# A product of the first MLP group is computed second, in a bank of its own, and operands read from PSUM are cut first

## The chip, the core and the metric

One core of a Trainium2 chip runs the whole kernel. The metric is the device time of one execution in microseconds (us); lower is better. Three runs of the kernel before gave 2158.07, 2158.14 and 2159.57 us; the median, 2158.14 us, is its time.

## What is computed

An encoder layer on 1536 tokens (512 and 1024) of width 1024: two kinds of attention, a gated merge, and an MLP with a squared ReLU. The change touches only the way into the MLP and its first product, `hn @ W_up`:

```python
hn = _rmsnorm(h, norm_mlp_g[l])
h = h + jnp.square(jax.nn.relu(hn @ w_mlp_up[l])) @ w_mlp_down[l]
```

All products are float32. The kernel writes each operand x as a rounded part hi and a remainder lo = x - hi, and adds three products, hi·hi + hi·lo + lo·hi (`mm3`, lines 190 to 193: L191, L192 and L193 in the profile).

## The kernel before

**Blocks and groups.** The MLP takes the tokens in two blocks of 768. For each block it runs through 16 groups of 256 hidden units. Within a group the product of a 2 by 2 block of weights with a 2 by 2 block of activations is built from seven smaller products instead of eight (Strassen's scheme in Winograd's form). The weights' halves are a11, a12, a21, a22 (`up_steps`, lines 1257 to 1284). From them and from the sums S0 to S3 come seven left operands A0 to A6, each cut into hi (L1212, on ScalarE, called ACT in the profile) and lo (L1213, on VectorE, called DVE). The right operands B0 to B6 are made once for a block by `pair_t` and stay for all its 16 groups.

**`pair_t`** (lines 310 to 349) makes three times 128 columns of B0 to B6. TensorE (PE) transposes two tiles of normalised activations into four PSUM banks (`pt`, L315). Two tiles of two banks each serve `pt` in the first block, and the next call's transposes must wait until the banks of the call before have been read for the last time. B0, B4 and B5 are bank contents as they stand (b11, b22, b21). B1, B2, B3 and B6 come from the differences a2, a1, a3, a4, which VectorE computes into SBUF (`ta`; L335, L334, L338, L340). y1 (L332) is a copy of the bank b12. `hi` (L324) rounds on ScalarE. `lo` (L327) subtracts on VectorE, for B2 and B6 on GpSimd (POOL). For the first block the three calls stand between the last matmuls of the output projection (`ops`), whose results also go to memory (`xrs`, L1149 on VectorE and L1150, a DMA that GpSimd issues).

**`up`** (lines 1292 to 1352) runs a group. Each of the seven products is 12 matmuls of 128x128 by 384 columns and adds into one of four PSUM banks, `ua`, `ub`, `uc`, `ud`. Their order is 0, 1, 2, 3, 4, 6, 5. Products 4, 6 and 5 are added onto a bank that held an earlier product, so they may start only when that one has been read: product 4 goes onto product 2's bank `uc` after s5 (L1343, ScalarE) has been copied from it, product 6 onto product 3's bank `ud` after L1330 (VectorE) has added it to s5, and product 5 onto product 0's bank `ua` after s1 (L1339) was copied. `put` adds (L1330), takes the ReLU and the square (L1331, L1332 on ScalarE) and stores. After each product `step` issues a share of the cuts for the next group (`side`).

**What sets the order.** The code is recorded, and a scheduler then places the instructions of each engine; what stands in one engine's queue is executed in that order. Loads are issued by SyncE (SP). The pool that holds A's cut operands (`k4`) lies where the projection's tiles lay, so a new tile of it may have to wait for the last use of what lay there, also for a store of `xrs` to land.

Of the kernel before, what the change touches and what calls it, by code (L numbers as in the profile page):

```python
# [15 lines left out]
ALU = mybir.AluOpType  # L16
# [14 lines left out]
HB = BT // 2  # L31
# [30 lines left out]
def encoder(ctx: ExitStack, tc: tile.TileContext, xs, outs, w):  # L62
    nc = tc.nc
# [126 lines left out]
    def mm3(out, ah, al, bh, bl, start, stop, **kw):  # L190
        nc.tensor.matmul(out, ah, bh, start=start, stop=False, **kw)  # L191
        nc.tensor.matmul(out, ah, bl, start=False, stop=False, **kw)  # L192
        nc.tensor.matmul(out, al, bh, start=False, stop=stop, **kw)  # L193
# [116 lines left out]
    def pair_t(nm, j, tiles, B, banks, tmp):  # L310

        b11, b21, b12, b22 = banks
        for halves, t in (((b11, b21), tiles[0]), ((b12, b22), tiles[1])):
            for c in range(NC8):
                nc.tensor.transpose(  # L315
                    halves[c // 4][:, (c % 4) * P : (c % 4 + 1) * P], t[:, c * P : (c + 1) * P], ident
                )
        cols = slice(j * P, (j + 1) * P)

        def v(t):  # L320
            return t.rearrange("p (k c) -> p k c", c=P)

        def hi(i, src):
            nc.scalar.activation(B[i][:, 0, :, cols], v(src), AF.Copy)  # L324

        def lo(i, src, eng=nc.vector):
            eng.tensor_tensor(B[i][:, 1, :, cols], v(src), B[i][:, 0, :, cols].bitcast(F32), op=ALU.subtract)  # L327

        y1 = tmp(f"y1{nm}")
        a2, a1, a3, a4 = (tmp(f"ta{i}{nm}") for i in (2, 1, 3, 4))  # L330
        hi(0, b11)
        nc.scalar.activation(y1, b12, AF.Copy)  # L332
        lo(0, b11)
        nc.vector.tensor_tensor(a1, y1, b11, op=ALU.subtract)  # L334
        nc.vector.tensor_tensor(a2, b22, a1, op=ALU.subtract)  # L335
        hi(1, a2)
        hi(2, a1)
        nc.vector.tensor_tensor(a3, b22, y1, op=ALU.subtract)  # L338
        hi(3, a3)
        nc.vector.tensor_tensor(a4, b21, a2, op=ALU.subtract)  # L340
        hi(4, b22)
        hi(5, b21)
        hi(6, a4)
        lo(4, b22)
        lo(5, b21)
        lo(1, a2)
        lo(2, a1, nc.gpsimd)
        lo(3, a3)
        lo(6, a4, nc.gpsimd)

    class Trunk:
        def __init__(self, sq, x, t0):
# [835 lines left out]
    def mlp():  # L1188
# [13 lines left out]
        def bank(name):  # L1202
            return ps.tile([P, 512], F32, tag="ps", name=name)

        def t2(name, shape=(P, 512), dt=F32):
            return k2.tile(list(shape), dt, tag="k2", name=name)
# [4 lines left out]
        def cut(hi, lo, src):  # L1211
            nc.scalar.activation(hi, src, AF.Copy)  # L1212
            nc.vector.tensor_tensor(lo, src, hi.bitcast(F32), op=ALU.subtract)  # L1213
# [43 lines left out]
        def up_steps(st, ops):  # L1257

            nm = f"{st[0]}_{st[1]}"
            raw = raw_up.pop(st)  # L1260
            a11, a21 = raw[0][:, :, 0:P], raw[0][:, :, P:FB]
            a12, a22 = raw[1][:, :, 0:P], raw[1][:, :, P:FB]
            S = {}

            def one(i):
                if i == 0 and st == (0, 0):
                    ops[0] = (first_a0[0][:, 0], first_a0[0][:, 1])
                    return
                t = k4.tile([P, 2, 4, P], F32R, tag="k4", name=f"A{nm}_{i}")
                if i in (1, 2, 3, 4) and not S:  # L1270
                    for n in (0, 1, 2, 3):
                        S[n] = t2(f"S{n}_{nm}", (P, 4, P))
                if i == 1:
                    nc.vector.tensor_tensor(S[0], a21, a22, op=ALU.add)
                    nc.vector.tensor_tensor(S[1], S[0], a11, op=ALU.subtract)  # L1275
                if i == 3:
                    nc.vector.tensor_tensor(S[2], a11, a21, op=ALU.subtract)
                if i == 4:
                    nc.vector.tensor_tensor(S[3], a12, S[1], op=ALU.subtract)
                src = {0: a11, 1: S.get(1), 2: S.get(0), 3: S.get(2), 4: S.get(3), 5: a12, 6: a22}[i]  # L1280
                cut(t[:, 0], t[:, 1], src)
                ops[i] = (t[:, 0], t[:, 1])

            return [lambda i=i: one(i) for i in (0, 1, 2, 3, 4, 6, 5)]

        late = []

        def run_late():
            while late:
                late.pop(0)()  # L1290

        def up(st, A, B, side):
            b, fb = st
            nm = f"{b}_{fb}"
            a, bk, c, d = (bank(f"u{n_}{nm}")[:, 0:HB] for n_ in "abcd")
            s1, s5, u2 = (t2(f"{n_}_{nm}")[:, 0:HB] for n_ in ("s1", "s5", "u2"))

            def step():
                if side:
                    for s in side.pop(0):  # L1300
                        s()

            def prod(out, i, bi, more):
                for k in range(4):
                    mm3(
                        out,
                        A[i][0][:, k, :],
                        A[i][1][:, k, :],
                        B[bi][:, 0, k, :],
                        B[bi][:, 1, k, :],  # L1310
                        k == 0 and not more,
                        k == 3,
                        skip_group_check=True,
                    )
                run_late()
                step()

            kept = {}

            def total(half):  # L1320
                t = t2(f"cs{half}_{nm}")[:, 0:HB]
                nc.vector.tensor_tensor(t, kept[0, half], kept[1, half], op=ALU.add)
                nc.sync.dma_start(ud[b][2][fb // 4][fb % 4, :, half * HB : (half + 1) * HB], t)

            def put(f, half, src, in1=None):
                t = t2(f"c{f}{half}_{nm}")[:, 0:HB]
                if in1 is None:
                    nc.scalar.activation(t, src, AF.Relu)
                else:
                    nc.vector.tensor_tensor(t, src, in1, op=ALU.add)  # L1330
                    nc.scalar.activation(t, t, AF.Relu)  # L1331
                nc.scalar.activation(t, t, AF.Square)  # L1332
                nc.scalar.dma_start(ud[b][f][fb // 4][fb % 4, :, half * HB : (half + 1) * HB], t)
                kept[f, half] = t
                if f == 0:
                    late.append(lambda: total(half))

            prod(a, 0, 0, False)
            nc.scalar.activation(s1, a, AF.Copy)  # L1339
            prod(bk, 1, 1, False)  # L1340
            nc.vector.tensor_tensor(u2, bk, s1, op=ALU.add)
            prod(c, 2, 2, False)
            nc.scalar.activation(s5, c, AF.Copy)  # L1343
            nc.vector.tensor_tensor(s5, s5, u2, op=ALU.add)
            prod(d, 3, 3, False)
            put(1, 1, d, s5)
            prod(c, 4, 4, True)
            put(0, 1, c, u2)
            prod(d, 6, 6, True)
            put(1, 0, d, u2)  # L1350
            prod(a, 5, 5, True)
            put(0, 0, a)

# [95 lines left out]
        def spread(steps, n):  # L1451

            q, r = divmod(len(steps), n)
            res, at = [], 0
            for i in range(n):
                k = q + (i < r)
                res.append(steps[at : at + k])
                at += k
            return res

        def run_up(b, A, B, last):

            for fb in range(NFB):
                An = {}
                if fb + 2 < NFB:
                    up_dma((b, fb + 2))
                side = up_steps((b, fb + 1), An) if fb + 1 < NFB else []
                side = side + last(fb)
                up((b, fb), A, B, spread(side, 7))
                A = An  # L1470

        def last_of(g):
# [38 lines left out]
        A, B = {}, B0  # L1511
        up_dma((0, 0))
        first_a = up_steps((0, 0), A)
        up_dma((0, 1))
        for s in first_a:
            s()
        run_up(0, A, B, last_0)
        run_late()


        A, B = {}, {}
        new_b(1, B)
        hn = {0: hn_load(1, 0)}
        for q in range(3):
# [17 lines left out]
            for i in range(2):  # L1542
# [3 lines left out]
                for r0 in (0, BT):  # L1546
                    nc.gpsimd.dma_start(hd[r0 + j * P : r0 + (j + 1) * P, 512:1024], t, accum_op=ALU.add)
        first_a = up_steps((1, 0), A)
        up_dma((1, 1))
        for s in first_a:  # L1550
            s()


        run_up(1, A, B, last_of(2))
        run_late()

# [65 lines left out]
        side = []  # L1622
        todo = []
        scales = []
        for i, (p, g, j) in enumerate(order):
            si = i // NTB
            if j == 0:
                if si + 2 < len(stages):
                    b_dma(*stages[si + 2], raw_k4)
                side = spread(b_steps(*stages[si + 1]), 5) if si + 1 < len(stages) else []  # L1630
# [19 lines left out]
            if g == NG - 1:  # L1650
                b, half = DEST[p][0]
# [83 lines left out]
```

## Time and profile before

| | |
|---|---|
| median of three runs | 2158.14 us (2158.07 to 2159.57) |
| the profiled execution's own time | 2156.44 us |
| its span, from first to last instruction | 2154.7 us |
| mean granted TensorE clock | 0.999 |
| TensorE matmuls | 10970 |

The profile gives for each engine the time that it was busy, and in a second view the instructions in order of time with start, duration, engine, line and operation. A row `x16` is sixteen equal instructions in a row. Matmuls overlap: each is listed with its full duration, and the distance from one start to the next is the time that PE spends on it. What stands in brackets is the idle time ahead of an instruction and what ended it. The stretch that matters here lies between 1188 us and 1262 us of the span: the three calls of `pair_t` for the first block, then the first groups of the MLP.

### The profile page before, as it was taken

The page shows a single profiled execution, that of the slowest core. Times are in us where ns is not written, and L with a number is a line of the kernel's source. Part 1 is how long each engine was busy: PE and PEld are TensorE (multiplying, and loading weights), DVE is VectorE, ACT ScalarE, POOL GpSimd, SP SyncE. Part 2 cuts the span into 40 slices and gives each one's busy share as a digit, 9 for nine tenths or more (in the row PEclk, how much of TensorE's full clock was granted, in tenths as well). Part 3 has the DMA queues.
Part 4 walks back from the last instruction along what each step waited for, and adds up shares of the span by engine and source line. Part 5 has one row for each costly group of instructions (what it writes and reads, how often), then busy time and mean ns, then how long its engine had stood idle before and what let it go on. Part 6 is the DMA issues. An engine that isn't in the chain of part 4 may idle for free. (4 is left out here: it accounts for less than half of the span.)

```text
span 2154.7 us, 31789 instructions
## 1 busy us (share of the span) xinstructions
PE 2120.7 (98%) x10970; PEld 1848.8 (86%) x10970; DVE 1475.6 (68%) x2801; ACT 1115.4 (52%) x2343; POOL 391.0 (18%) x506
## 2 busy tenths in 40 slices
PE   8999999899999999999999999999999999999998
PEld 7787878888898888887888899998999988888886
DVE  6665786777666754656882877778777777769563
ACT  5654653556646654555540566566555643434352
POOL 2232420332233314433300200003000000000000
PEclk9999999999999999999999999999999999999999
DMA  5435557520122133433463655578445799688561
GB/s 166 146 105 169 151 171 254 190 75 24 48 78 79 42 92 90 126 100 99 154 209 118 213 182 179 184 232 229 144 157 157 244 353 340 218 285 279 166 199 65
DMA packets 319578, 350.91 MB, mean 163 GB/s; under 512 B 31160, under 2 KB 255032, under 8 KB 319417
## 3 DMA queue, kind: packets, MB, share of 16 engines
q1 hardware_dynamic: 277927, 279.65, 41.3%
q10 hardware_dynamic: 35810, 52.19, 6.9%
q0 software_dynamic: 5680, 17.04, 2.8%
q8 instruction: 87, 1.43, 0.3%
q14 instruction: 74, 0.61, 0.1%
HBM read 264.85 MB, written 87.88 MB: 164 GB/s over the span
## 5 line engine op out<-in xcount | busy, mean ns | idle before, releaser
L193 PE MATMUL dn<-wd,al 128*128 128x512 f32 x624 | 242.8, 389 | 0.0
L192 PE MATMUL dn<-wd,ah 128*128 128x512 f32 x624 | 242.8, 389 | 0.0
L191 PE MATMUL dn<-wd,ah 128*128 128x512 f32 x624 | 242.7, 389 | 0.0
L1212 ACT ACTIVATE ah<-ar 128x512 fp32r<-128x512 f32 x168 | 104.4, 628 | 205.2 <-PE dn L192 191.3
L1213 DVE TENSOR_TENSOR al<-ar,ah 128x512 fp32r<-128x512 f32 x168 | 115.1, 691 | 77.5 <-ACT ah L1212 66.4
L192 PEld LDWEIGHTS dn<-wd,ah 128*128 128x128 f32 x624 | 117.2, 188 | 24.4
L191 PEld LDWEIGHTS dn<-wd,ah 128*128 128x128 f32 x624 | 117.2, 188 | 24.2
L193 PEld LDWEIGHTS dn<-wd,al 128*128 128x128 f32 x624 | 117.2, 188 | 24.2
L681 POOL TENSOR_SCALAR ps<-ps,rls 128x1024 f32<-128x1024 f32 (+1 forms) x96 | 97.2, 1013 | 215.7 <-DVE rls L680 198.7
L721 DVE TENSOR_TENSOR ptls<-pTs,pths 128x512 fp32r<-128x512 f32 x160 | 107.6, 686 | 38.0 <-ACT pths L720 37.4
L720 ACT ACTIVATE pths<-pTs 128x512 fp32r<-128x512 f32 x160 | 94.2, 598 | 73.9 <-PE pTs L715 71.7
L675 DVE TENSOR_REDUCE nms<-ss 128x1 f32<-128x1024 f32 (+1 forms) x96 | 99.9, 1041 | 25.4 <-PE ss L673 25.0
L176 POOL TENSOR_TENSOR rs_f<-ms_f,mhalf 128x1 f32<-128x1 f32 x6 | 4.0, 668 | 590.7 <-DVE ms_f L172 590.7
L191 PE MATMUL gpss<-xs_0h,w_gs 128*128 128x512 f32 x256 | 104.7, 409 | 0.3 <-ACT w_gs L180 0.2
L678 ACT ACTIVATE ps<-ss,nms 128x1024 f32<-128x1024 f32 (+1 forms) x96 | 93.3, 973 | 22.4 <-DVE nms L675 20.0
L715 PEld LDWEIGHTS pTs<-ident,ps 128*128 128x128 f32 x640 | 78.2, 140 | 28.2 <-POOL ps L681 4.2
L193 PE MATMUL gpss<-xs_0h,w_gs 128*128 128x512 f32 x256 | 100.9, 394 | 0.0
L192 PE MATMUL gpss<-xs_0l,w_gs 128*128 128x512 f32 x256 | 100.8, 394 | 0.0
L715 PE MATMUL pTs<-ident,ps 128*128 128x128 f32 x640 | 98.9, 274 | 1.3 <-DVE ptls L721 0.6
L1212 ACT ACTIVATE A<-S 128x512 fp32r<-128x512 f32 x128 | 75.9, 623 | 30.7 <-DVE S L1275 23.4
L191 PE MATMUL ud<-B,A 128*128 128x384 f32 x256 | 85.7, 335 | 1.6 <-DVE c L1330 1.6
L1213 DVE TENSOR_TENSOR A<-S,A 128x512 fp32r<-128x512 f32 x128 | 84.5, 686 | 4.0 <-ACT A L1212 3.9
(325 smaller groups left out, 6369.8 us busy)
## 6 DMA issues: line engine op xcount, KB each, us to landing
ar<-ud SPq DMA_DIRECT2D x120, 512.0 KB
br<-in_w_mlp_down_dram SPq DMA_DIRECT2D x72, 512.0 KB
rawu<-in_w_mlp_up_dram SPq DMA_DIRECT2D x64, 512.0 KB
ud<-c ACTq DMA_DIRECT2D x128, 192.0 KB
raw_gs<-in_w_in_dram SPq DMA_DIRECT2D x32, 512.0 KB
zgs<-sgs ACTq DMA_DIRECT2D x48, 256.0 KB
ud<-cs SPq DMA_DIRECT2D x64, 192.0 KB
raw_os<-in_w_out_dram SPq DMA_DIRECT2D x16, 512.0 KB
```

The lines of the kernel that those rows point to most:

```text
L176: nc.gpsimd.tensor_tensor(r[:, :n], m[:, :n], mhalf[:, :n], op=ALU.pow)
L191: nc.tensor.matmul(out, ah, bh, start=start, stop=False, **kw)
L192: nc.tensor.matmul(out, ah, bl, start=False, stop=False, **kw)
L193: nc.tensor.matmul(out, al, bh, start=False, stop=stop, **kw)
L675: nc.vector.tensor_reduce(nm_, s, axis=AX.X, op=ALU.max, negate=True)
L678: nc.scalar.activation(p, s, AF.Exp, bias=nm_, accum_out=l)
L681: nc.gpsimd.tensor_scalar(p, p, rl, 1.0, op0=ALU.mult, op1=ALU.mult)
L715: nc.tensor.transpose(pt[:, j * P : (j + 1) * P], PP[u, j][:, kc * P : (kc + 1) * P], ident)
L720: nc.scalar.activation(hi, pt, AF.Copy)
L721: nc.vector.tensor_tensor(lo, pt, hi.bitcast(F32), op=ALU.subtract)
L1212: nc.scalar.activation(hi, src, AF.Copy)
L1213: nc.vector.tensor_tensor(lo, src, hi.bitcast(F32), op=ALU.subtract)
```

## The change

It has three parts. In `pair_t`, B4 (read from PSUM) is rounded right after y1's subtraction, and the differences and cuts follow in another order: both lo parts that read PSUM (B4, B5) now stand ahead of the lo parts that read SBUF (B1, B3). In the first group of the first block alone, product 5 is computed second, into a fifth bank `ue`, and put at once with s1 as its second summand; the last product of the group falls away from its old place, and the sum of the two parts of a half (`total`) is queued once both are there. Its left operand A5 is therefore cut right after A0. In that group the cuts for the next group begin two products later (`[[], []] + spread(side, 5)` in place of `spread(side, 7)`).

```diff
         hi(0, b11)
         nc.scalar.activation(y1, b12, AF.Copy)
         lo(0, b11)
         nc.vector.tensor_tensor(a1, y1, b11, op=ALU.subtract)
+        hi(4, b22)
+        hi(2, a1)
         nc.vector.tensor_tensor(a2, b22, a1, op=ALU.subtract)
-        hi(1, a2)
-        hi(2, a1)
+        lo(2, a1, nc.gpsimd)
+        nc.vector.tensor_tensor(a4, b21, a2, op=ALU.subtract)
+        hi(5, b21)
         nc.vector.tensor_tensor(a3, b22, y1, op=ALU.subtract)
-        hi(3, a3)
-        nc.vector.tensor_tensor(a4, b21, a2, op=ALU.subtract)
-        hi(4, b22)
-        hi(5, b21)
         hi(6, a4)
         lo(4, b22)
+        lo(6, a4, nc.gpsimd)
         lo(5, b21)
+        hi(1, a2)
+        hi(3, a3)
         lo(1, a2)
-        lo(2, a1, nc.gpsimd)
         lo(3, a3)
-        lo(6, a4, nc.gpsimd)
...
-            return [lambda i=i: one(i) for i in (0, 1, 2, 3, 4, 6, 5)]
+            return [lambda i=i: one(i) for i in ((0, 5, 1, 2, 3, 4, 6) if st == (0, 0) else (0, 1, 2, 3, 4, 6, 5))]
...
-                if f == 0:
+                if (1 - f, half) in kept:
                     late.append(lambda: total(half))
...
             nc.scalar.activation(s1, a, AF.Copy)
+            if st == (0, 0):
+                e = bank(f"ue{nm}")[:, 0:HB]
+                prod(e, 5, 5, False)
+                put(0, 0, e, s1)
             prod(bk, 1, 1, False)
...
-            prod(a, 5, 5, True)
-            put(0, 0, a)
+            if st != (0, 0):
+                prod(a, 5, 5, True)
+                put(0, 0, a)
...
-                up((b, fb), A, B, spread(side, 7))
+                if (b, fb) == (0, 0):
+                    side = [[], []] + spread(side, 5)
+                else:
+                    side = spread(side, 7)
+                up((b, fb), A, B, side)
```

How the instructions then stand, at three places. The first is VectorE in the first call of `pair_t`, between the subtraction a1 and the next projection result. `ta` is each of the differences, `pt_0_0` holds b11 and b21, `pt_0_1` holds b12 and b22. The line numbers move by a few since lines were added.

```order
-L335 TENSOR_TENSOR ta_0_12838<-pt_0_1_12820,ta_0_12839 128x512
-L338 TENSOR_TENSOR ta_0_12840<-pt_0_1_12820,y_0_12837 128x512
-L340 TENSOR_TENSOR ta_0_12841<-pt_0_0_12819,ta_0_12838 128x512
+L337 TENSOR_TENSOR ta_0_12838<-pt_0_1_12820,ta_0_12839 128x512
+L339 TENSOR_TENSOR ta_0_12841<-pt_0_0_12819,ta_0_12838 128x512
+L341 TENSOR_TENSOR ta_0_12840<-pt_0_1_12820,y_0_12837 128x512
+L327 TENSOR_TENSOR B_4_12811<-pt_0_1_12820,B_4_12811 128x4x128
+L327 TENSOR_TENSOR B_5_12812<-pt_0_0_12819,B_5_12812 128x4x128
 L327 TENSOR_TENSOR B_1_12808<-ta_0_12838,B_1_12808 128x4x128
 L327 TENSOR_TENSOR B_3_12810<-ta_0_12840,B_3_12810 128x4x128
-L327 TENSOR_TENSOR B_4_12811<-pt_0_1_12820,B_4_12811 128x4x128
-L327 TENSOR_TENSOR B_5_12812<-pt_0_0_12819,B_5_12812 128x4x128
```

The lo parts of B4 and B5 moved up by two places, ahead of those of B1 and B3, and a4 ahead of a3.

The second place is PE around the transposes of the second call, among the matmuls of the projection (`ops_1_5`). This is how it stands now:

```order
L191 MATMUL ops_1_5_12942<-wh_os_1_0_12422,mgs_1_0_0_12042 128x512
L315 MATMUL pt_1_0_12894<-ident,hn_1_12861 128x128 x8
L315 MATMUL pt_1_1_12895<-ident,hn_4_12863 128x128 x8
L192 MATMUL ops_1_5_12942<-wl_os_1_0_12423,mgs_1_0_0_12042 128x512
L193 MATMUL ops_1_5_12942<-wh_os_1_0_12422,mgs_1_0_1_12043 128x512
L191 MATMUL ops_1_5_12942<-wh_os_1_0_12422,mgs_1_0_0_12042 128x512
L192 MATMUL ops_1_5_12942<-wl_os_1_0_12423,mgs_1_0_0_12042 128x512
L193 MATMUL ops_1_5_12942<-wh_os_1_0_12422,mgs_1_0_1_12043 128x512
L191 MATMUL ops_1_5_12942<-wh_os_1_4_12434,mgs_1_4_0_12222 128x512
```

Before, the two rows L315 stood five matmuls later, just ahead of the row with `wh_os_1_4`. In the third call they moved up by five matmuls in the same way.

The third place is ScalarE at the start of the first group: first as it stood, from the last cut of `pair_t`, then as it stands now. `A_0_5` is A5 of the first group, `A_1_0` A0 of the second; `s_0_0` from `ua` is s1 and from `uc` is s5.

```order
L324 ACTIVATE B_6_12813<-ta_2_12994 128x4x128
L1212 ACTIVATE A_0_1_13126<-S_0_0_13128 128x512
L1212 ACTIVATE A_0_2_13135<-S_0_0_13127 128x512
L1212 ACTIVATE A_0_3_13138<-S_0_0_13129 128x512
L1212 ACTIVATE A_0_4_13142<-S_0_0_13130 128x512
L1212 ACTIVATE A_0_6_13146<-rawu_0_1_13120 128x512
L1212 ACTIVATE A_0_5_13149<-rawu_0_1_13120 128x512
L1212 ACTIVATE A_1_0_13175<-rawu_1_0_13122 128x512
L1339 ACTIVATE s_0_0_13160<-ua_0_13156 128x384
L1343 ACTIVATE s_0_0_13161<-uc_0_13158 128x384
L1212 ACTIVATE A_1_1_13191<-S_0_1_13193 128x512
L1212 ACTIVATE A_1_2_13213<-S_0_1_13192 128x512
```

```order
L1212 ACTIVATE A_0_4_13145<-S_0_0_13133 128x512
L1212 ACTIVATE A_0_6_13149<-rawu_0_1_13120 128x512
L1339 ACTIVATE s_0_0_13160<-ua_0_13156 128x384
L1212 ACTIVATE A_1_0_13206<-rawu_1_0_13122 128x512
L1331 ACTIVATE c_0_0_13189<-c_0_0_13189 128x384
L1332 ACTIVATE c_0_0_13189<-c_0_0_13189 128x384
L1333 DMA ud_0_0_13090<-c_0_0_13189 128x384
L1212 ACTIVATE A_1_1_13209<-S_0_1_13211 128x512
L1212 ACTIVATE A_1_2_13231<-S_0_1_13210 128x512
L1347 ACTIVATE s_0_0_13161<-uc_0_13158 128x384
L1212 ACTIVATE A_1_3_13234<-S_0_1_13212 128x512
```

The cut of A5 now comes first, ahead of A1 to A3 (not shown). The copy s5, for which product 4 waits, now stands behind the cuts A1 and A2 of the second group instead of ahead of them. On PE the first group's products now run 0, 5, 1 and 2 (mixed), 3, then five matmuls of the second group's product 0, then 4, five more of that product 0, and 6. From the fifth group of the first block on the order is as before, but for the cuts in the three calls of `pair_t` for the second block.

## The prediction

> **What bounds the kernel now.** I read the page's first lines first, for the busy shares and the clock.
>
> ```profile
> span 2154.7 us, 31789 instructions
> PE 2120.7 (98%) x10970; PEld 1848.8 (86%) x10970; DVE 1475.6 (68%) x2801; ACT 1115.4 (52%) x2343; POOL 391.0 (18%) x506
> PEclk9999999999999999999999999999999999999999
> ```
>
> PE is busy for 98% of the span and its clock is full in every slice. The change neither adds nor removes a matmul: the product that comes second falls away at its old place. So only time in which PE stands still can be won. The second view is what PE waits for between 1190 and 1240 us (tile and line waiting, what ends the wait; us, times, longest).
>
> ```profile
> PE ud L191 <- DVE c L1330: 1.6, 1, 1.6
> PE pt L315 <- DVE B L327: 0.8, 1, 0.8
> PE ub L191 <- ACT A L1212: 0.7, 1, 0.7
> ```
>
> There are three waits, and each is one that the change moves something for. The third view, PE's timeline, gives their size including the short stops that the list of waits leaves out.
>
> ```profile
> 1194.97 0.39 PE L191 MATMUL ops<-wh_os,mgs 128*128 128x512 f32 x1
> 1195.20 0.39 PE L192 MATMUL ops<-wl_os,mgs 128*128 128x512 f32 x1
> ...
> 1196.11 0.39 PE L193 MATMUL ops<-wh_os,mgs 128*128 128x512 f32 x1
> 1197.25 1.97 PE L315 MATMUL pt<-ident,hn 128*128 128x128 f32 x16 [0.76 <-DVE B L327]
> ...
> 1204.09 1.91 PE L315 MATMUL pt<-ident,hn 128*128 128x128 f32 x16
> ...
> 1214.48 0.33 PE L191 MATMUL ua<-B,A 128*128 128x384 f32 x1
> ...
> 1217.47 0.44 PE L191 MATMUL ub<-B,A 128*128 128x384 f32 x1 [0.72 <-ACT A L1212]
> ...
> 1228.24 0.44 PE L191 MATMUL ud<-B,A 128*128 128x384 f32 x1 [1.60 <-DVE c L1330]
> ...
> 1232.53 0.33 PE L191 MATMUL ua<-B,A 128*128 128x384 f32 x1
> 1234.61 0.33 PE L191 MATMUL ub<-B,A 128*128 128x384 f32 x1
> ...
> 1247.09 0.33 PE L191 MATMUL ua<-B,A 128*128 128x384 f32 x1
> ```
>
> A projection matmul takes 0.23 us from start to start (1194.97 to 1195.20). So the transposes of the second call could start at 1196.11 + 0.23 = 1196.34; they start at 1197.25, **0.91 us** late. The third call's (1204.09) show no wait. The first group runs from 1214.48 to 1232.53, 18.05 us. The second, with as many matmuls, takes 14.56 us (1232.53 to 1247.09), 14.56 / 84 = 0.173 us each and 2.08 a product. The first group therefore loses **3.49 us**. Together that is 4.40 us, 0.20% of the time, and the most that the change can win here. For the second block it moves the same cuts, but there the transposes do not wait:
>
> ```profile
> 1451.38 1.47 PE L315 MATMUL pt<-ident,hn 128*128 128x128 f32 x12
> ```
>
> The row shows no idle time in brackets, so there is nothing to be won, and cuts that free the banks earlier give no reason for one: I cost this block at 0.
>
> **Part 1, `pair_t` in the first block.** VectorE's timeline:
>
> ```profile
> 1192.42 0.68 DVE L335 TENSOR_TENSOR ta<-pt,ta 128x512 f32<-128x512 f32 x1
> 1193.02 0.68 DVE L338 TENSOR_TENSOR ta<-pt,y 128x512 f32<-128x512 f32 x1
> 1193.62 0.68 DVE L340 TENSOR_TENSOR ta<-pt,ta 128x512 f32<-128x512 f32 x1
> 1194.22 2.38 DVE L327 TENSOR_TENSOR B<-ta,B 128x512 fp32r<-128x512 f32 x2
> 1196.52 1.28 DVE L327 TENSOR_TENSOR B<-pt,B 128x512 fp32r<-128x512 f32 x2
> 1199.01 0.69 DVE L327 TENSOR_TENSOR B<-pt,B 128x512 fp32r<-128x512 f32 x1 [0.62 <-ACT B L324]
> ...
> 1215.29 0.68 DVE L1274 TENSOR_TENSOR S<-rawu,rawu 128x512 f32<-128x512 f32 x1
> 1216.01 0.69 DVE L1275 TENSOR_TENSOR S<-S,rawu 128x512 f32<-128x512 f32 x1
> ```
>
> Independent instructions of 128x512 start 0.60 us apart (1192.42, 1193.02), and 0.72 where one needs the other's result (1215.29, 1216.01). The lo of B4, the first row at 1196.52, ends at 1197.20 and releases the transposes. Now a2 is followed by a4, which needs it (1193.14), a3 (1193.74), and then the lo of B4: 1194.34 to 1195.02, 2.18 us earlier. The transposes moved up by five projection matmuls, so PE reaches them at 1196.34 - 5 x 0.227 = 1195.20. By then the banks are free; their second half is due eight transposes later, at about 1196.1, and the lo of B5 ends at 1195.62. The wait of 0.91 goes.
>
> What is late next could be the third call. PE reaches it 0.91 earlier through the lost wait and 1.14 through the five matmuls, at 1204.09 - 2.05 = 1202.04. VectorE begins the second call's cuts, at 1199.01 before, about one us earlier: the four lo parts and one `xrs` that it does first end near 1198.0. From there it is a1 1198.6, a2 1199.3, a4 1200.0, a3 1200.6, and the lo of B4 from 1201.2 to 1201.9, in time by about 0.1. The other input is the last `hn` load. SyncE's row and the DMA view from 1195 to 1205 us, in forty slices of 0.25 us:
>
> ```profile
> 1198.37 0.33 SPq L1042 DMA_DIRECT2D hn<-hnd  x1
> ```
>
> ```profile
> GB/s 451 410 410 418 418 279 98 16 33 0 0 0 0 0 0 123 205 393 385 385 311 311 246 279 295 377 344 279 213 33 16 0 0 0 0 33 0 0 0 0
> ```
>
> The load is issued at 1198.37, in a queue whose order stays. Its half of the transposes is due at 1202.04 + 0.87 = 1202.91, where before it was due at 1204.96 and not late. The traffic that begins with it at 1198.75 ends at about 1202.7, so it may have landed just in time. The bounds are a loss of 0 and of 1204.96 - 1202.91 = 2.05; I take 0.1, near the lower end, by that row. Part 1 is worth 0.91 - 0.1, about **0.8 us**.
>
> At one place a rule bears on this order. These rows are POOL's beside VectorE's:
>
> ```profile
> 1194.44 1.61 POOL L327 TENSOR_TENSOR B<-ta,B 128x512 fp32r<-128x512 f32 x1 [2.86 <-ACT B L324]
> 1196.44 1.29 POOL L327 TENSOR_TENSOR B<-ta,B 128x512 fp32r<-128x512 f32 x1 [0.39 <-ACT B L324]
> ```
>
> While POOL worked at 1194.44, VectorE's two lo parts with both operands in SBUF took 2.38 us. While it worked at 1196.44, the two that read PSUM took 1.28 us, no longer than alone. The Trainium skill (SBUF — State Buffer, "Who interferes with whom") says that a VectorE instruction with two SBUF inputs contends with a GpSimd instruction that reads SBUF, and that one with at most one SBUF input does not; the trace agrees, with 2.38 against 1.28. By that rule the lo of B4 and B5, moved beside POOL's work, keep their 0.60 and the sum below stands; if they were held too, the lo of B4 in the second call would end about 1.1 later and the whole gain would be about 2.4.
>
> **Part 2, the first group.** I count from its start, X = 1214.48 before. What ScalarE and VectorE did:
>
> ```profile
> 1216.79 2.19 ACT L1212 ACTIVATE A<-S 128x512 fp32r<-128x512 f32 x4 [5.40 <-PE ua L193]
> 1220.49 1.68 ACT L1212 ACTIVATE A<-rawu 128x512 fp32r<-128x512 f32 x3 [1.50 <-issue]
> 1222.07 0.47 ACT L1339 ACTIVATE s<-ua 128x384 f32<-128x384 f32 x1
> ```
>
> ```profile
> 1227.63 0.55 DVE L1330 TENSOR_TENSOR c<-ud,s 128x384 f32<-128x384 f32 x1
> ```
>
> Before, product 1 (`ub`) was due at X + 2.08 but its A1 was not cut until 1216.79. Now product 5 fills X + 2.08 to 4.16; its A5 is cut from a loaded tile, needs none of the sums, and is first in the queue. Product 1 is due at X + 4.16 = 1218.64, when A1 and its lo part are there. These stops, 3.49 - 1.60 = 1.9, go.
>
> Products 1 and 2 then run to X + 8.32, product 3 to 10.40, and five matmuls of the next group to 11.27. Next is product 4, which waits for s5. ScalarE held at 1220.49 = X + 6.01 for a place in `k4`, the fifth after A1 to A3 and A5, that a store of `xrs` had to free. The fifth is now A4, so I leave that time: A4 6.01, A6 6.54, s1 7.07 to 7.6 (0.53 a cut, 1.68 for three). From there VectorE adds the new c00 (7.9 to 8.45, 0.55 as at L1330), then a lo part from 8.35, S0 8.95, S1 9.67 to 10.35; ScalarE cuts A1 and A2 of the next group at 10.4 and 10.9 and only then copies s5, 11.45 to 11.95. Product 4 starts 0.7 late and, like the rows at 1217.47 and 1228.24, loses 0.1 more on the restart: **0.8 us, a new wait** that comes from c00 and the cuts ahead of s5. The cover that hid s5 was its place ahead of these cuts.
>
> Product 4 ends at about X + 14.15 and five matmuls at 15.02. Product 6 needs the c of L1330, which came at 1227.63 = X + 13.15. Behind s5 it is now about 14.35 to 14.9: in time, with 0.1 to spare. Its wait of 1.60 goes. Product 6 ends at 17.1, two matmuls are left, and the next group's product 1 starts at X + 17.45, where before it was 1234.61 = X + 20.13. Part 2 wins **2.7 us**. After that VectorE has room:
>
> ```profile
> 1232.50:1247.10 14.60, 14.60 (x87) 14.60 (x86) 11.64 (x20) 9.62 (x19) 0.00 (x0) 1.00 0.49 159
> ```
>
> In the windows view (length; busy PE, PE's loads, VectorE, ScalarE, POOL; clock; DMA share; GB/s) the second group has VectorE busy for 11.64 of 14.60 us, so I cost the cuts that were put off by two products at nothing; without that cover the next group's first cuts would be late by a part of 0.6 each.
>
> **The sum.** 0.8 + 2.7 = 3.5 us. The profiled execution took 2156.44 us (span 2154.7 and 1.74 around it): 2151.2 and 2152.9. The median of the runs is 1.70 above it, so 2158.14 - 3.5 = **2154.6 us**. A measurement of this kernel can tell about 0.2%, 4.3 us, from no change; the forecast lies within that, and so it counts as the same.
>
> **The rivals.**
> - *The wait goes to the third call.* `hn` lands, or the lo of B4 ends, 1 to 2 us after PE asks (the margins are 0.1). For it: SyncE's queue does not move. Against it: the traffic ends at 1202.7. Gain 1.5 to 2.6, 2155.5 to 2156.6. Chance 0.17.
> - *No stall is left.* If the 1.50 us that ScalarE idled behind the store shrinks, or A1 of the next group is cut sooner, product 4 finds s5 in time. Gain 4.4, 2153.7, just over 0.2%. Chance 0.14.
> - *Won here, lost later.* PE gets ahead and waits for the next load instead, so the time stays near 2158. Against it: the second group has no wait. Chance 0.05.
> - *Slower, through the store.* The critical chain shows the store ahead of that cut:
>
> ```profile
> 1215.67 3.32 DMA hd<-xrs
> 1218.99 1.50 issue
> 1220.49 0.64 ACT A L1212
> ```
>
> It released the cut 4.82 us after its issue. Now A4, A6, s1, s5 and the sums behind them all follow it, so each us that it comes later costs product 4 one us. From 3.5 us later (8.3 after issue) the kernel is slower than before, and over 0.2% slower from 12.6 after issue. Stores of `xrs` here landed after 4.6 us in the median and 7.3 at most:
>
> ```profile
> hd<-xrs POOLq DMA_DIRECT2D x4, 256.0 KB, 4.6
> ```
>
> Chance 0.05, most of it near 2159 to 2161.
>
> **How the numbers follow.** The forecast, 2153.8 to 2155.5, gets 0.59. The range takes in the full gain with the spread of a median below it (2152.9) and the first rival above it (to 2157.0). Faster by over 0.2% needs the second rival's full 4.4 us and gets 0.13, about its chance; slower by over 0.2% gets 0.04 of the last rival's 0.05; the same gets 0.83.
>
> **What would show it.** Right: no wait at the transposes of the second call, `ue` starting 2.1 us after `ua` and `ub` 4.2 after, a wait of 0.5 to 1 us at product 4 put down to s5 on ScalarE, none at product 6, and the second group's `ub` 17.5 us after X. Wrong: a wait of over 0.5 us at the third call's transposes, a cut of A4 more than 7 us after X, a wait at product 6, or a new one in the second or third group.

## The result, and the profile after

Nine runs of the changed kernel had a median of 2152.99 us (2152.14 to 2155.4), nine of the kernel before 2158.14; the ratio is 0.9981, with a 95% interval of 0.9972 to 0.9989. Eleven more runs of it, beside 33 of the kernel before, gave 2154.07 against 2157.80 us and a ratio of 0.9984 (0.9975 to 0.9993). So by the two ratios the change makes the kernel 3.4 to 4.1 us faster, 0.16 to 0.19%; the intervals allow 1.5 to 6.0 us, and the medians by themselves lie 5.15 and 3.73 us apart. The forecast was 3.5 us and 2154.6 us. The first median, 2152.99, lies below the band 2153.8 to 2155.5 that had the largest chance and only just above 2152.9, the lower end of the forecast's range; the second, 2154.07, lies in the band.

The head of the page after:

```profile
span 2150.9 us, 31794 instructions
PE 2121.0 (99%) x10970; PEld 1850.6 (86%) x10970; DVE 1474.0 (69%) x2802; ACT 1116.2 (52%) x2343; POOL 388.4 (18%) x506
```

PE does the same work in a span that is 3.8 us shorter. PE's timeline after (start, duration, operation) has the rows that answer to those of before:

```profile
1186.68 1.91 PE L315 MATMUL pt<-ident,hn 128*128 128x128 f32 x16
...
1195.47 1.91 PE L315 MATMUL pt<-ident,hn 128*128 128x128 f32 x16
...
1202.01 0.39 PE L192 MATMUL ops<-wl_os,mgs 128*128 128x512 f32 x1
1202.47 2.03 PE L315 MATMUL pt<-ident,hn 128*128 128x128 f32 x16
...
1214.14 0.33 PE L191 MATMUL ua<-B,A 128*128 128x384 f32 x1
...
1216.25 0.33 PE L191 MATMUL ue<-B,A 128*128 128x384 f32 x1
...
1218.33 0.33 PE L191 MATMUL ub<-B,A 128*128 128x384 f32 x1
...
1225.43 0.33 PE L191 MATMUL uc<-B,A 128*128 128x384 f32 x1
...
1228.38 0.33 PE L191 MATMUL ud<-B,A 128*128 128x384 f32 x1
...
1230.81 0.33 PE L191 MATMUL ub<-B,A 128*128 128x384 f32 x1
...
1234.97 0.33 PE L191 MATMUL ud<-B,A 128*128 128x384 f32 x1
```

None of these rows has idle time in brackets. The second call's transposes do not wait. `ue` starts 2.11 us and `ub` 4.19 us after X = 1214.14, product 4 (`uc`) at X + 11.29, where it is due, product 6 (`ud`) at X + 14.24, and the second group's `ub` at X + 16.67. Predicted were 17.45 and a wait of 0.8 us at product 4: that wait does not exist. ScalarE's rows show why. A1 to A4 are cut in one row without a stop, and s5, the copy that product 4 waits for, is done at X + 10.87:

```profile
1216.92 2.20 ACT L1212 ACTIVATE A<-S 128x512 fp32r<-128x512 f32 x4 [4.66 <-DVE S L1275]
...
1224.54 0.47 ACT L1347 ACTIVATE s<-uc 128x384 f32<-128x384 f32 x1
```

The span differs from execution to execution ahead of the change, so I compare by places in the program. T is the start of the first call's transposes, Z the start of the second group's product 3. From Z to the end of the span every kernel here took 915.8 to 915.9 us: what is won before Z is neither lost nor added to later. T itself lay anywhere from 1186.2 to 1189.2.

| kernel | T to X | X to the fifth cut | X to Z | T to Z | won |
|---|---|---|---|---|---|
| before, two profiles | 28.07, 28.08 | 6.01, 5.81 (A6) | 24.29, 24.10 | 52.36, 52.18 | |
| changed, two profiles | 27.46, 27.50 | 4.37 (A4) | 20.83 | 48.29, 48.33 | 3.96 |
| helper's part alone | 27.35 | 4.41 (A6) | 23.40 | 50.75 | 1.52 |
| first group's part alone | 28.07 | 5.98 (A4) | 21.67 | 49.74 | 2.53 |
| the same, load gbl behind the store | 28.07 | 4.45 (A4) | 20.83 | 48.90 | 3.37 |

The column "won" is against 52.27, the mean of the two profiles of before. "The fifth cut" is the one that takes the place in `k4` which the last store of `xrs` must free: A6 before, A4 now. The fourth cut of a row `x4` is put at three times its spacing, 0.53 us, behind the row's start.

### The profile page after: what moved, and what is told of

Same layout as the page of the kernel before. It is cut to its first block, busy times and chain, and to the rows that moved or that the text cites. A ratio compares the mean times of both kernels' runs of the same rounds, so it can differ in the third digit from the quotient of the medians.

```text
span 2150.9 us, 31794 instructions
## 1 busy us (share of the span) xinstructions
PE 2121.0 (99%) x10970; PEld 1850.6 (86%) x10970; DVE 1474.0 (69%) x2802; ACT 1116.2 (52%) x2343; POOL 388.4 (18%) x506
## 4 chain that ended last, share of the span: by engine, by line
PE 81%; DVE 3%; issue 1%; ACT 1%; POOL 1%; DMA 1%; SPq 0%; ACTq 0%; POOLq 0%; DVEq 0%
PE dn L192 6%; PE dn L191 6%; PE dn L193 6%; PE pTs L715 3%; PE gpss L193 2%; PE gpss L191 2%; PE gpss L192 2%; PE ud L191 2%; PE uc L191 2%; PE ud L193 2%; PE uc L193 2%; PE uc L192 2%; PE ud L192 2%; PE ua L191 2%; PE ua L193 2%; PE ua L192 2%
## 5 line engine op out<-in xcount | busy, mean ns | idle before, releaser
L1331 ACT ACTIVATE c<-c 128x384 f32<-128x384 f32 x97 | 50.7, 524 | 68.4 <-DVE c L1330 68.4
```

## The experiments

**Both kernels once more.**

> The kernel before, unchanged, profiled once more. X is the start of the first MLP group's first matmul. Theory A (the store of xrs lands late because of what is queued ahead of it): the cut of A6 again comes 4 to 5 us after the last store of xrs is issued, product 6 again waits 1.3 to 1.8 us, and X to the second group's ub is again near 20.1 us. Theory B (that 1.50 us idle time was an accident of one execution): the cut of A6 comes 3.0 to 3.5 us after the issue and X to ub is about 19.

The cut of A6 came 4.63 us after the store's issue, after 1.31 us of idle time; product 6 waited 1.42 us, and X to the second group's `ub` was 19.94 us. These are the numbers of theory A: the idle time that only read "issue" in the first profile comes again and belongs to the kernel. Why the store lands late, this run does not tell. The ratio was 0.9999 (0.9990 to 1.0008).

> The changed kernel, unchanged, profiled and timed once more. Both theories: X to the second group's ub 16.7 us, no wait at product 4 or 6, 0.2 to 0.4 us lost at the third call's transposes. If its gain comes only from the stops counted in the first block it is 3.8 to 4.4 us against before; if the gain is 5 us or more, something outside of the first block has gained too.

X to `ub` was 16.67 us and there was no wait; the third call cost 0.23 us before its transposes and 0.18 in them. The gain is 3.96 us by the trace and 3.4 us by the ratio: nothing outside the first block is needed to explain it.

**Each part alone.**

```diff
 # the helper's part alone: pair_t as changed, up_steps, up and run_up as before
 # the first group's part alone: the other way round
```

> Only the new order in the helper for the right operands; the first group as before. Both theories: no wait at the second call's transposes, about 0.3 us lost at the third call's, so X comes 0.6 us earlier; ub still waits for A1, 0.7 us in one piece. Theory A (this part also issues the stores of xrs and the load gbl on POOL earlier, so the last store lands sooner): the cut of A6 comes 3.0 to 3.5 us after the store's issue instead of 4.8, product 6 waits under 0.6 us instead of 1.6, and the whole gain is 1.6 to 2.1 us. Theory B (the first group knows nothing of this part): product 6 waits 1.6 us as before and the gain is 0.6 us.

PE's and ScalarE's timelines of this kernel (X = 1215.23; POOL issued the store at 1216.42):

```profile
1218.22 0.44 PE L191 MATMUL ub<-B,A 128*128 128x384 f32 x1 [0.72 <-ACT A L1212]
...
1228.13 0.44 PE L191 MATMUL ud<-B,A 128*128 128x384 f32 x1 [0.72 <-DVE c L1330]
```

```profile
1217.54 2.19 ACT L1212 ACTIVATE A<-S 128x512 fp32r<-128x512 f32 x4 [6.41 <-PE ua L193]
1219.64 1.66 ACT L1212 ACTIVATE A<-rawu 128x512 fp32r<-128x512 f32 x3
```

The wait for A1 stayed as it was. The cut of A6 follows the others with no idle time, 3.22 us after the store's issue, and product 6 waits 0.72 us instead of 1.60, a little more than the 0.6 that theory A allowed. The part won 0.73 us before X and 0.80 us behind it, in a group that it does not touch; together 1.52, where theory A gave 1.6 to 2.1 and theory B 0.6. So it is theory A, a little smaller than expected: the two parts are coupled. The ratio, 0.9994 (0.9985 to 1.0003), is too wide to show 1.5 us by itself.

> Only the first group's part (product 5 second in a bank of its own, its put, the later cuts); the helper for the right operands as before. Both theories: the second call's transposes wait 0.8 us as before, ue and ub start 2.1 and 4.2 us after X. Theory A: the store lands as late as before, A4 is cut 5.5 to 6.1 us after X, s5 is copied near X + 11.4, product 4 waits 0.5 to 0.9 us, and the gain is 2.7 us. Theory B: A4 comes at X + 4.4, product 4 does not wait, X to the second group's ub is 16.7 us and the gain is 3.4 us.

X is 1217.22 here, and the store was issued at 1218.41:

```profile
1220.09 1.68 ACT L1212 ACTIVATE A<-S 128x512 fp32r<-128x512 f32 x3 [4.75 <-DVE S L1275]
1223.20 0.63 ACT L1212 ACTIVATE A<-S 128x512 fp32r<-128x512 f32 x1 [1.43 <-DMA hd<-xrs]
...
1228.71 0.47 ACT L1347 ACTIVATE s<-uc 128x384 f32<-128x384 f32 x1
```

```profile
1229.23 0.44 PE L191 MATMUL uc<-B,A 128*128 128x384 f32 x1 [0.55 <-ACT s L1347]
```

This is the predicted schedule: A4 waits for the store until X + 5.98 (predicted 6.01), s5 is copied at X + 11.49 (11.45), product 4 starts 0.7 us late, and the second group's `ub` comes at X + 17.51 (17.45). So the chain was worked out rightly, but for the wrong kernel: with the helper's part as well, A4 does not wait. The ratio was 0.9991 (0.9982 to 1.0000).

**Why the store lands late.** POOL's timelines of before, of after, and of the first group's part alone, in three fences:

```profile
1214.77 0.54 POOL L1240 DMA_DIRECT2D gbl<-in_norm_mlp_g_dram  x1
1215.67 0.55 POOL L1150 DMA_DIRECT2D hd<-xrs  x1 [0.35 <-DVE xrs L1149]
```

```profile
1213.38 0.54 POOL L1240 DMA_DIRECT2D gbl<-in_norm_mlp_g_dram  x1
1215.33 0.54 POOL L1150 DMA_DIRECT2D hd<-xrs  x1 [1.41 <-DVE xrs L1149]
```

```profile
1217.51 0.54 POOL L1240 DMA_DIRECT2D gbl<-in_norm_mlp_g_dram  x1
1218.41 0.55 POOL L1150 DMA_DIRECT2D hd<-xrs  x1 [0.35 <-DVE xrs L1149]
```

The store is tied to the last projection matmul and comes at X + 1.2 in all three. The load gbl (512 KB) stands in POOL's queue behind the third store, which follows VectorE's third addition, and that one comes after the third call's cuts. The changed helper ends those cuts sooner against X, so gbl is issued 1.95 us ahead of the last store instead of 0.90. The profile also lists the time from the issue of this store to its landing, and it follows that distance: 4.6 to 4.7 us with gbl 0.90 ahead (both profiles of before, and the first group's part alone), 2.9 to 3.0 with gbl 1.83 to 1.98 ahead (the changed kernel twice, and the helper's part alone). Three experiments ask whether gbl is what delays the store. The first two did not answer it as meant.

```diff
 # first group's part alone
-                    nc.gpsimd.dma_start(gl[0], ...)
-                    late_load(late_norms[0])
+                    hl[late_norms[0]] = raw4(...)
...
+            if st == (0, 1):
+                nc.gpsimd.dma_start(gl[0], ...)
+                nc.gpsimd.dma_start(hl[late_norms[0]], ...)
```

> The first group's part alone, as in the run of it, but on POOL's queue the 512 KB load gbl and the last store of xrs change places; every other order is as there. Theory A (the store lands late because that load is queued 0.9 us ahead of it): the store lands within 3.2 us of its issue, A4 is cut at X + 4.4 in one row with A1 to A3, product 4 does not wait, X to the second group's ub goes from 17.5 to 16.7 us. Theory B (the store's lateness comes from other traffic, such as the loads of the up weights that SyncE issues): A4 again near X + 6.0, 17.5 us.

It is inconclusive. The order of the queues was as planned, but tiles in memory changed places, so the second load of the up weights had to wait for another tile, and A5 itself was late:

```profile
1217.52 0.64 ACT L1212 ACTIVATE A<-rawu 128x512 fp32r<-128x512 f32 x1 [4.42 <-DMA rawu<-in_w_mlp_up_dram]
```

That load (X was 1216.19) then fell on the stores, whose median to landing rose to 5.6 us. The last store took 5.2 us to land with gbl 0.78 us behind it, so gbl isn't the only traffic that can hold it. X to the second group's `ub` was 18.04 us and the ratio 0.9993 (0.9984 to 1.0003).

```diff
 # first group's part alone
-                        (nc.gpsimd if later else nc.scalar).dma_start(hd[rows_, hc], xr)
+                        (nc.gpsimd if later and tt != 7 else nc.scalar).dma_start(hd[rows_, hc], xr)
```

> The first group's part alone, with the last store of xrs issued by ScalarE instead of POOL, so that it no longer stands behind the load gbl in POOL's queue; the loads of the up weights, gbl and everything else stay where they are. Theory A (the store is late because of what stands ahead of it in its own queue): A4 is cut in one row with A1 to A3, by X + 4.6, product 4 does not wait, and X to the second group's ub is 16.7 to 16.9 us instead of 17.5. Theory B (it is late because all transfers share the engines with gbl and the weights): A4 is cut at X + 5.5 or later and 17.2 to 17.6 us remain.

```profile
1217.73 0.33 ACTq L1150 DMA_DIRECT2D hd<-xrs  x1
...
1222.75 0.64 ACT L1212 ACTIVATE A<-S 128x512 fp32r<-128x512 f32 x1 [0.84 <-DMA hd<-xrs]
```

From a queue of its own the store still released A4 only 5.02 us after its issue, at X + 5.94, and X to `ub` was 17.46 us. Theory A in that form falls: its place behind gbl in POOL's queue is not the cause. What remains, not yet shown by this run, is that the transfers get in each other's way wherever they are issued. The 17.46 is not the store's doing alone: with the store's issue ahead of A5 in ScalarE's queue, A5 and A1 came later and `ub` started at X + 4.60 instead of 4.19. And the load `hl` (512 KB), which POOL issues right behind the store elsewhere, now went out 0.11 us ahead of it. The ratio was 0.9984 (0.9974 to 0.9993), not distinguishable from that of the first group's part alone.

```diff
 # first group's part alone
-                    nc.gpsimd.dma_start(gl[0], ...)
-                    late_load(late_norms[0])
+                    nc.gpsimd.memset(gl[0][:, :, 0:8], 0.0)
+                    hl[late_norms[0]] = raw4(...)
+                    nc.gpsimd.memset(hl[late_norms[0]][:, 0:8], 0.0)
...
+            if st == (0, 2):
+                nc.gpsimd.tensor_copy(gl[0][:, 0, 8:16], raw_up[0, 1][0][:, 0, 0:8])
+                nc.gpsimd.tensor_copy(hl[late_norms[0]][:, 8:16], raw_up[0, 1][0][:, 0, 0:8])
+                nc.gpsimd.dma_start(gl[0], ...)
+                nc.gpsimd.dma_start(hl[late_norms[0]], ...)
```

> The first group's part alone, as in its run, with the load gbl (512 KB) issued behind the last store of xrs on POOL's queue instead of 0.9 us ahead of it; this time the weights' loads keep their places and their order (POOL writes a few elements of the two tiles early, so that they hold their place in memory). Theory A (the transfer of gbl takes the DMA engines from the store, in whatever queue the store is): the store lands within 3.2 us of its issue, A4 is cut with A1 to A3 by X + 4.8, product 4 waits under 0.2 us, X to the second group's ub is 16.7 to 16.9 us instead of 17.5. Theory B (gbl has no part in it): A4 at X + 5.5 or later, product 4 waits 0.5 us or more, 17.2 us or more.

X is 1216.34:

```profile
1217.53 0.54 POOL L1150 DMA_DIRECT2D hd<-xrs  x1 [0.74 <-DVE xrs L1149]
...
1219.02 0.54 POOL L1259 DMA_DIRECT2D gbl<-in_norm_mlp_g_dram  x1
```

```profile
1219.20 2.20 ACT L1212 ACTIVATE A<-S 128x512 fp32r<-128x512 f32 x4 [4.75 <-POOL hl L1258]
```

With gbl out of the store's way, A1 to A4 are cut in one row, A4 3.26 us after the store's issue; product 4 does not wait, and X to `ub` is 16.67 us, the same as in the changed kernel. The store landed 2.3 us after its issue. (The bracket names POOL's copy, but A1 comes at X + 2.86, as in the first group's part alone.) So without gbl close ahead of the store A4 isn't held, and the first group's part gives its full 3.37 us. The edit also moved `hl`, from 0.54 us behind the store to 2.03. That `hl` alone is the cause is ruled out: in the changed kernel it stands 0.53 us behind the store and A4 is in time, and with gbl 2.36 us ahead (the run with a3 moved, below) the store landed after 2.4 us beside the same `hl`. Whether gbl close ahead is enough without `hl` was not tried. The ratio was 0.9982 (0.9973 to 0.9992).

**What a late store costs.**

```diff
 # changed kernel; in the second run one such store instead of two
+                        if nxt is None and half == 1 and tt == 7:
+                            for q in range(2):
+                                nc.gpsimd.dma_start(dram.tile([P, 512], F32, name=f"more{q}"), xr)
                         (nc.gpsimd if later else nc.scalar).dma_start(hd[rows_, hc], xr)
```

> The changed kernel, with the last projection result also stored twice to a scratch place ahead of its own store (256 KB each on POOL's queue). That store is issued 1.1 us later and lands later still. The five matmuls of the second group that stood ahead of product 4 now stand behind it, so product 4 is due at X + 10.4. Theory A (as the prediction has it, the cut of A4 waits for that store, and s5 and product 4 follow it in ScalarE's queue): wherever A4 is cut, product 4 starts 6.0 us after it; with A4 at X + 7 to 9 that is X + 13 to 15, and the kernel loses 2.6 to 4.6 us against the changed kernel, each us one us, so that it is about as slow as before. Theory B (A4's lateness is taken up by the idle time ahead of s5): product 4 waits under 1 us and the loss is under 1 us.

> As the run with the store put later, with one extra store of 256 KB ahead of it instead of two; the order of all engines is otherwise the same as there. Both theories: product 4 starts 6.0 us after the cut of A4. A4 then comes at X + 5.2 to 6.2, product 4 is due at X + 10.4 and waits 0.8 to 1.8 us. Theory A (the slow matmuls seen there, 0.32 us apart at a granted clock of 0.54, follow only a long enough stop; before, after 1.60 us they were 0.18 apart): with a wait of up to 1.6 us no slow stretch, and the loss against the changed kernel is the wait plus 0.1 to 0.2, 1.0 to 1.8 us. Theory B (the slow stretch belongs to the place or to the extra traffic): the matmuls of product 4 are slow again and 1.6 us more are lost.

With two extra stores A4 was cut at X + 6.65 and product 4 started at X + 12.62, 5.97 us later; with one, at X + 5.79 and X + 11.76, again 5.97 later. Between the two runs each us of the store cost product 4 one us, as the prediction had it. With two stores A4 came earlier than the X + 7 to 9 that was expected. X to Z rose to 24.72 and 22.72 us, a loss of 3.89 and 1.89. The first lies in the expected 2.6 to 4.6 by luck, since the wait made only 2.0 of it; the second is just above the expected 1.0 to 1.8. The loss of 1.89 is the 1.2 us that product 4 waited, a stop of 0.3 ahead of product 6, and restarts. Of the loss of 3.89, most of what goes beyond the wait is in PE's rows behind it:

```profile
1226.93 0.49 PE L191 MATMUL uc<-B,A 128*128 128x384 f32 x1 [1.87 <-ACT s L1350]
1227.21 0.53 PE L192 MATMUL uc<-B,A 128*128 128x384 f32 x1
1227.53 0.53 PE L193 MATMUL uc<-B,A 128*128 128x384 f32 x1
...
1230.67 0.34 PE L191 MATMUL ua<-B,A 128*128 128x384 f32 x1
```

The twelve matmuls of product 4 took 3.74 us instead of 2.08. The windows view (its column before the last two is the granted clock) shows that TensorE ran slower:

```profile
1226.90:1230.60 3.70, 3.67 (x12) 3.67 (x13) 2.83 (x6) 1.81 (x4) 0.00 (x0) 0.54 0.46 142
```

TensorE was granted 0.54 of its clock for these 3.7 us. With one extra store, after a wait of 1.03 us, product 4 took 2.20. So the slow matmuls did not come back, as theory A of that run has it, but that is one case on each side, and the last section shows that the length of a stop alone does not decide. The times were 2157.46 us, ratio 1.0001 (0.9992 to 1.0011), with two extra stores, and 2155.78, 0.9994 (0.9984 to 1.0004), with one. So A4 cut 2.3 us later than now undoes nearly the whole change (T to Z is 52.07 against 52.27 before); 0.9 us of that belong to the order of these two kernels, in which five matmuls that could fill the wait stand behind product 4.

**The put-off cuts.**

```diff
-                if (b, fb) == (0, 0):
-                    side = [[], []] + spread(side, 5)
-                else:
-                    side = spread(side, 7)
+                side = spread(side, 7)
```

> The changed kernel without its third part: the cuts for the second group are spread over all seven products again, none is put off. Theory A (the put-off is needed, since the cuts of the second group stand ahead of s5 and of the sum that product 6 waits for): a wait of 0.5 to 1 us at product 4 or 6, X to the second group's ub 17.2 to 17.7 us. Theory B (with A4 cut at X + 4.4 there is room for them): no wait at product 4 or 6 and the same PE time; the first group costs nothing more, within 0.3 us.

PE waited nowhere in the first block, and X to Z was 20.83 us, the same to the last digit as in the changed kernel. (X to the second group's `ub` was 14.59, as two of its matmuls then stand ahead of product 6.) The ratio was 0.9986 (0.9976 to 0.9995). Theory B: with A4 cut early, this part of the change is worth nothing here. Whether it would matter with a late store wasn't tried.

**The third call's transposes.**

```diff
-        nc.vector.tensor_tensor(a3, b22, y1, op=ALU.subtract)
         hi(6, a4)
         lo(4, b22)
         lo(6, a4, nc.gpsimd)
         lo(5, b21)
+        nc.vector.tensor_tensor(a3, b22, y1, op=ALU.subtract)
```

> The changed kernel with the difference a3 moved behind the lo parts of B4 and B5, so these come one VectorE instruction (0.6 us) earlier in each call. Theory A (only the lo of B4 makes the third call's transposes late): their start moves 0.16 us earlier, they take 1.91 us and X comes 0.16 to 0.35 us earlier against the first call's transposes (27.1 to 27.3 us instead of 27.48). Theory B (their second half waits for the last hn load anyway): the start moves, the second half stops for 0.3 us or more instead of 0.12 to 0.18, and X stays at 27.4 to 27.5.

T to X was 27.34 us. That is between the two theories, and no less than in four other kernels with the changed helper as it is (27.34 to 27.35), so nothing was won that stands out; the ratio was 0.9981 (0.9970 to 0.9991). The scheduler also drew the transposes' halves apart, with matmuls of the projection between them, so it does not tell what their second half waited for; that stays open.

## Why the prediction came out as it did

- **What bounds the kernel** was right: PE's matmuls did not change, and the gain is PE's waits. Of the 4.40 us counted as the most, 3.96 came, and none of it was given back behind Z. Only "its clock is full in every slice" reads too much into the row of nines: a 9 stands for 90% or more, and in this trace the granted clock was 0.50 from 404.10 to 407.50 us. In the stretch of the change it was full.
- **Part 1, the second call's wait.** Right: from T to the second call's transposes PE took 10.84 us before and 8.79 after; the 2.05 is 0.91 and the five matmuls' 1.14, as worked out.
- **Part 1, the third call.** Right in kind, too small: 0.1 was taken, and in the first profile 0.35 was lost, so that T to X is shorter by 0.6, not 0.8. (0.06 came back in the second call, whose transposes took 1.91 us instead of 1.97.) The matmul ahead of the third call's transposes started at 1202.01, so they could have started at 1202.24; they started at 1202.47, 0.23 late. VectorE's rows show where this comes from:

```profile
1198.88 0.67 DVE L334 TENSOR_TENSOR ta<-y,pt 128x512 f32<-128x512 f32 x1
1199.69 0.69 DVE L337 TENSOR_TENSOR ta<-pt,ta 128x512 f32<-128x512 f32 x1
1200.48 0.69 DVE L339 TENSOR_TENSOR ta<-pt,ta 128x512 f32<-128x512 f32 x1
...
1201.69 1.28 DVE L327 TENSOR_TENSOR B<-pt,B 128x512 fp32r<-128x512 f32 x2
```

  From a1 to a2 and from a2 to a4 it took 0.81 and 0.79 us, not the 0.72 taken from the sums' rows. In the first call a2 to a4 did take 0.72; but the trace of before has 0.80 from a1 to a2 in the second call (1199.88 to 1200.68), a row that the prediction did not use. The lo of B4 ended at 1202.37, and the transposes followed. The rest, 0.03 to 0.18, is in the transposes themselves (1.94 to 2.09 us instead of 1.91) and varied between executions.
- **The rule on operands read from PSUM** was tested by half: the moved lo parts of B4 and B5 took 1.28 us for two, as the row shows, but POOL's cut of B6 began only at 1202.40, when the lo of B4 was done. So only the lo of B5 ran beside POOL, and it was not held up.
- **Part 2, products 5 and 1 and product 6's wait.** Right: all of these stops went.
- **Part 2, product 4's wait.** This step failed. The prediction wrote: "The fifth is now A4, so I leave that time: A4 6.01". The time was taken from a schedule in which gbl was moving beside the store, and part 1 moves gbl. The two parts were costed one beside the other, and the sum lacked the link between them. With part 2 alone the numbers of the step came out (A4 at X + 5.98, s5 at 11.49, `ub` at 17.51); with both, A4 is cut at X + 4.37 and the 0.8 us are not lost. In place of the forecast came the rival "no stall is left", by the first of its two ways, the shrinking idle time behind the store.
- **The size.** 3.5 against 3.96 by the trace: 0.2 too much in part 1, 0.7 too little in part 2. That the total came so close is partly luck, since the two errors have opposite signs.
- **The slower rival** had the right mechanism and too low a price: the wait costs us for us, but in the run with two extra stores a wait of 2.0 us was followed by a lower clock, which cost 1.66 us more. It was priced to break even with A4 3.5 us behind X + 6.0; with the order that the scheduler then chose, it nearly broke even at X + 6.65.

## What to carry to other kernels

Two edits in neighbouring stages are not two separate sums. Follow what the first one does to the queues between them, DMA issues included, before a wait in the second is given its old time. And a wait that the profile puts down to "issue" has a cause: find which transfer the waiting instruction needs, and what else is on the DMA engines then; here a load that nothing was waiting for yet held back a store that PE's product hung on.

## What the runs showed of the hardware

- A 256 KB store released its waiter 4.6 to 5.0 us after issue with a 512 KB load begun 0.6 to 0.9 us ahead, from POOL's queue (4.82, 4.63, 4.79) and from ScalarE's (5.02) alike, and 3.3 us or less after issue where that load came 1.5 us later or 1.8 to 2.4 us ahead. (In the run from ScalarE's queue a second load of 512 KB went out 0.11 us ahead of the store as well.) The Trainium skill (DMA: Bandwidth & Descriptors, "Anatomy of one DMA — SWDGE (gpsimd) path") gives about 2.0 us of fixed time plus the bytes at 436 GB/s; an estimate by that page is 2.6 us. The stores with the load behind them landed after 2.3 us in the median of two, 0.3 less than it; the one close behind the load, 4.6 to 4.7, does not agree with it.
- A stop of PE of 2.0 us (1.87 in the list of waits) was followed by 3.7 us at a granted clock of 0.54; stops in the same place listed with 1.60, 1.42 and 1.03 us were not. The length alone does not decide. A stop near 402 us, listed with 1.74 us in both profiles of before, was followed by half the clock in the first and by the full clock in the second:

```profile
404.10:407.50 3.40, 2.94 (x12) 2.43 (x11) 2.60 (x8) 1.47 (x5) 2.73 (x5) 0.50 0.57 179
```

```profile
404.10:407.50 3.40, 2.32 (x15) 2.00 (x14) 2.75 (x8) 1.47 (x6) 2.73 (x4) 1.00 0.53 168
```

  In the thirteen profiles of this case that stop was followed by such a stretch seven times, and a stop of 2.13 us near 315 us (the run with a3 moved) was not. What else decides stays open.
- Identical instructions ahead of T ended anywhere from 1186.2 to 1189.2 us. From 300 to 500 us the granted clock was 1.00 in the earliest (before, second profile) and 0.98 in the latest (first group's part alone), where PE also stood for 3.48 us near 315 us. This scatter is nearly as large as the gain, so changes of this size are better read between two places in the program than from spans. What makes all of it wasn't shown.
